# A hybrid encoder of two layers: the builder orders the whole program by a model of five queues, and B's second values are projected ahead of its second queries

## The chip, the cores and the metric

The kernel runs on one core of one Trainium2 chip. The metric is the device time of one execution in microseconds (us). TensorE (PE) multiplies matrices, VectorE (DVE), ScalarE (ACT) and GpSimd (POOL) do the rest, and SyncE (SP) issues the DMAs. Each engine has a queue of its own, and the engines signal each other by semaphores.

## The reference

x has 512 positions of 1024 features, in float32; there are two layers. Cut to what matters:

```python
h = rmsnorm(x, g_attn[l])
qa, ka, va, qb, kb, vb = split(h @ w_in[l])
# q and k: RMSNorm per head of 64, then rotary
ya = windowed_gqa_sink(qa, ka, va, sink[l])     # A: 8 q heads, 2 kv heads, window +-128, a sink logit
yb = diff_attention(qb, kb, vb, lam)            # B: 4 heads, (softmax(q0 k0) - lam softmax(q1 k1)) v
yb = rmsnorm(yb, subln[l]) * (1.0 - lambda_init)
x = x + concat(ya, yb) @ w_out[l]
h = rmsnorm(x, g_ffn[l])
gate, val = split(h @ w_up[l])                  # 2816 columns each
x = x + (silu(centred_dwconv(gate)) * val) @ w_down[l]
```

## The kernel before

Every product of weights is made of three matmuls (`mm3`, L228 to L231): each operand is split into a high part in a shortened float format and a low part, the rest, and high x high, high x low and low x high are added up. Weights come in units (L178 to L194) of 128 partitions x up to 1024 elements by a DMA on SP into two raw buffers; ACT casts the high part and DVE or POOL subtracts the low part (`emit_unit`, L198). `next_unit` keeps up to three units ahead. For the later input weights and the output weights POOL makes the low part in four quarters (L213), for the others DVE does in one piece (L219).

A layer goes in these stages:

- **Projections** (`project`, L355). The columns of w_in are nine chunks of 256 (`CHUNKS`, L29): akv (A's keys and values), aq0 and aq1, then B by halves: bq0, bk0, bv0, bq1, bk1, bv1. Each takes two units and 4 x 8 x 3 = 96 matmuls of 256 columns, and fills two PSUM banks (512 columns of a float each) in turn. The norm's scale per position, na_r, is applied when a bank is emptied: `scaled` (L373) for queries and keys, `v_out` (L437) for values. `qk_out` (L376) then does the norm per head and the rotary (for B on POOL), transposes on PE and splits.
- **Group A**, eight steps of (ip, qb): `a_scores` (sc_a, L507), `a_soft` (exponentials L534, scales L546 and L549), `a_values` (transposes pt_a L578, copies p_a L554 and L556, products pv_a). Four of eight `tmp` buffers belong to a step, so two steps are under way at most.
- **Group B**, sixteen scores of (half, qb, j): `b_scores` (sc_b, L638) into one pair of banks that there is once, `b_soft` (maximum L648, exponentials L654, the difference L663), `b_weights` (transposes wt_b L682), `b_values` (yb), and `b_norm` after every four (ss_yb L721, rr_yb L273, rt_yb L735). The queries and keys of the second half take the buffers of A's queries, so bq1 comes after A's last score.
- **Output projection**: `out_pass` 0 for A, 1 for B's first half, and `out_last` for the second half by halves of the positions (wo, L817).
- **Channel mixer** (L859 to L903): 22 steps of two up products (gate and value, 24 matmuls of 512 columns each) with a chain of nine operations on DVE, ACT and POOL, and two down passes of 8 products. Over both layers that is 88 up units and 64 down units.

The order of the attention part comes from `pump` (L142). The scores, the values and the projections with the output passes (`filler`, L830) are generators; each yields how long it thinks its matmuls took, or a condition on `clk["now"]`. The ready one of lowest rank goes on (values 1, scores 2, filler 3, all side work 0). Blocks of filler are up to 1.45 us long by this clock. What the side work costs on ACT, DVE and POOL stands in `pause` and `mark` as constants. The rest of the program is put out stage by stage in program order. The framework, called with schedule_with_timeline_sim=True (L957), then schedules what it was given; the trace shows single matmuls of one product between those of another.

At the start the squares of the first norm (L254) are scaled by `gate`, a value 1.0 that is computed from the low part of the fourth weight unit (L303), so that they come after it. In layer 0 akv is multiplied slice by slice as x and its weights arrive (L294 to L300).

Of the kernel before, what the change touches and what calls it, by code (L numbers as in the profile page):

```python
# [28 lines left out]
CHUNKS = ("akv", "aq0", "aq1", "bq0", "bk0", "bv0", "bq1", "bk1", "bv1")  # L29
CW = 256  # L30
AHEAD = 3
# [3 lines left out]
FIRST_MM = 1  # L35
N_COL = NK + NK + 3 * NF + NF + 1
N_ROW = 4 * HD + 8 + 4 * HD


@with_exitstack  # L40
def kernel(
# [17 lines left out]
    PSUM = bass.MemoryType.PSUM  # L59

    const = ctx.enter_context(tc.tile_pool(name="const", bufs=1))
# [3 lines left out]
    def pair(name):  # L65
        return sb.tile([P, 2, S], F32R, tag="pair", bufs=8, name=name)

    def keep(name):
        return sb.tile([P, 2, S], F32R, tag="keep", bufs=10, name=name)

    def hid(name, part):
        return sb.tile([P, S], F32R, tag=f"hid{part}", bufs=NK, name=name)

    def prob(name):
        return sb.tile([P, 2, S], F32R, tag="prob", bufs=4, name=name)

    def tmp(name, n=S):
        return sb.tile([P, S + 16], F32, tag="tmp", bufs=8, name=name)[:, :n]

    def rp(name):  # L80
        return sb.tile([P, 2, CW], F32, tag="rp", bufs=RP, name=name)
# [7 lines left out]
    def mm(name):  # L89
        return ps.tile([P, S], F32, tag="mm", bufs=2, name=name)  # L90

    def at(name):
        return ps.tile([P, S], F32, tag="at", bufs=2, name=name)

    def sc2(name):
        return ps.tile([P, 2, S], F32, tag="sc", bufs=1, name=name)

    def accum(name):
        return ps.tile([P, S], F32, tag="acc", bufs=1, name=name)

    def tq(name):
        return ps.tile([P, S], F32, tag="tq", bufs=1, name=name)

    cyc = {"i": 0}

    def wide(name):
        cyc["i"] += 1
        i = cyc["i"] % 5
        return sc2(name)[:, 0] if i == 4 else (mm, at)[i % 2](name)

    def turn(name):
        cyc["i"] += 1
        return (mm, at)[cyc["i"] % 2](name)

    def run(gen):
        for _ in gen:
            pass

    def chain(*gens):
        for g in gens:  # L120
            yield from g


    never = 1e9
    clk = {"now": 0.0}
    due = {}
    tracks = []

    def pause(dt):
        t = clk["now"] + dt  # L130
        return lambda: t

    def when(*names):
        return lambda: max(due.get(n, never) for n in names)

    def mark(name, dt=0.0):
        due[name] = clk["now"] + dt

    def spawn(rank, gen):
        tracks.append([rank, gen, lambda: 0.0])  # L140

    def pump():  # L142
        while tracks:
            ready = [v for v in tracks if v[2]() <= clk["now"]]
            if not ready:
                clk["now"] = min(v[2]() for v in tracks)
                assert clk["now"] < never
                continue
            tr = min(ready, key=lambda v: v[0])
            step = next(tr[1], None)  # L150
            if step is None:
                tracks.remove(tr)
            elif callable(step):
                tr[2] = step
            else:
                clk["now"] += step
                tr[2] = lambda: 0.0
# [9 lines left out]
    ones, nhalf, warm, gate, zero = (unit[:, i:i + 1] for i in range(5))  # L167
# [8 lines left out]

# [18 lines left out]
    state = {"emitted": 0, "used": 0}  # L195
    ready = []
    
    def emit_unit():  # L198
        i = state["emitted"]
        src, (k, n), kind = units[i]  # L200
        raw = sb.tile([P, k, n], F32, tag="wr", bufs=2, name=f"wr{i}")
        hi = sb.tile([P, k, n], F32R, tag="wh", bufs=3, name=f"wh{i}")
        lo = sb.tile([P, k, n], F32R, tag="wl", bufs=3, name=f"wl{i}")
        nc.sync.dma_start(raw, src)
        eng = nc.gpsimd if kind in ("inb", "out") else nc.vector
        if eng is nc.vector:
            split(eng, hi, lo, raw)
        else:
            nc.scalar.copy(hi, raw)  # L209
            q = k // 4  # L210
# [3 lines left out]
        ready.append((hi, lo))  # L214
        state["emitted"] += 1

    def split(eng, hi, lo, raw):
        nc.scalar.copy(hi, raw)  # L218
        eng.tensor_tensor(out=lo, in0=raw, in1=hi, op=ALU.subtract)  # L219

    def next_unit():
        while state["emitted"] < min(len(units), state["used"] + 1 + AHEAD):
            emit_unit()
        u = ready[state["used"]]
        state["used"] += 1
        return u

    def mm3(acc, a, b, start, stop):  # L228
        nc.tensor.matmul(acc, lhsT=a[0], rhs=b[0], start=start, stop=False)  # L229
        nc.tensor.matmul(acc, lhsT=a[0], rhs=b[1], start=False, stop=False)  # L230
        nc.tensor.matmul(acc, lhsT=a[1], rhs=b[0], start=False, stop=stop)  # L231


    class Norm:
        def __init__(self, l, base, name):
            self.l, self.base, self.name = l, base, name
            self.x = []
# [3 lines left out]
            self.part = sb.tile([P, S], F32, tag="tab", bufs=3, name=f"{name}_sum")  # L241

        def add(self, k, x):
            g = cols[:, self.l, self.base + k:self.base + k + 1]
            self.hi[k] = hid(f"{self.name}_h{k}", 0)
            self.lo[k] = hid(f"{self.name}_l{k}", 1)
            nc.scalar.activation(self.hi[k], x, AF.Copy, scale=g)
            nc.vector.scalar_tensor_tensor(out=self.lo[k], in0=x, scalar=g, in1=self.hi[k],  # L248
                                           op0=ALU.mult, op1=ALU.subtract)
            self.x.append(x)  # L250

        def square(self, k):
            sq = self.part if k == 0 else tmp(f"{self.name}_q{k}")
            nc.scalar.activation(sq, self.x[k], AF.Square, **({"scale": gate} if self.first else {}))  # L254
            if k:
                eng = nc.gpsimd if self.base == 0 and not self.first else nc.vector
                eng.tensor_tensor(out=self.part, in0=self.part, in1=sq, op=ALU.add)

        def rms(self):
            acc = accum(f"{self.name}_ss")  # L260
            for t in range(NT):
                nc.tensor.matmul(acc[:, t:t + 1], lhsT=self.part[:, t * P:(t + 1) * P], rhs=ones,
                                 start=True, stop=True)
            v = small(f"{self.name}_v", NT)
            nc.vector.tensor_scalar(out=v, in0=acc[:, 0:NT], scalar1=1.0 / D, scalar2=EPS,
                                    op0=ALU.mult, op1=ALU.add)
            r = small(f"{self.name}_r", NT)
            rsqrt(r, v)
            return r

    def rsqrt(o, i):
        e = nhalf if len(i.shape) == 2 else nhalf.unsqueeze(2)
        nc.gpsimd.tensor_tensor(out=o, in0=i, in1=e.broadcast_to(list(i.shape)), op=ALU.pow)  # L273

    def split_out(hi, lo, src):
        split(nc.vector, hi, lo, src)

    nc.scalar.activation(warm, ones, AF.Copy, scale=ones)
    nc.sync.dma_start(cols[:, :, :N_COL], col_par)
    first_w = [[sb.tile([P, 4, CW], dt, tag=tag, bufs=b, name=f"{tag}_f{i}")  # L280
                for dt, tag, b in ((F32, "prob", 4), (F32R, "wh", 3), (F32R, "wl", 3))] for i in range(2)]
    for k in range(NK):
        nc.sync.dma_start(x_sb[k], x_v[:, k])
        nc.sync.dma_start(first_w[k // 4][0][:, k % 4], units[k // 4][0][:, k % 4])
    state.update(emitted=2, used=2)
    ready.extend([None, None])
    nc.sync.dma_start(ident, ident_in)
    norm = Norm(0, 0, "na0")
    first_banks = []
    for tp in range(2):  # L290
        b = mm(f"pj0_akv_{tp}")
        nc.tensor.matmul(b, lhsT=zero.broadcast_to([P, P]), rhs=zero.broadcast_to([P, S]), start=True, stop=False)
        first_banks += [b[:, i * CW:(i + 1) * CW] for i in range(2)]
    for k in range(NK):  # L294
        norm.add(k, x_sb[k])
# [10 lines left out]
    for k in range(NK):  # L306
        norm.square(k)

    for l in range(depth):
# [19 lines left out]
        if l:  # L329
            make_tabs((2, 3))  # L330
# [130 lines left out]
        def first_part():  # L461
# [7 lines left out]
            else:  # L469
# [5 lines left out]
                for _ in range(3):  # L475
                    yield next(g)
# [496 lines left out]
```

## Time and profile before

| what | us |
|---|---|
| three runs: median (lowest, highest) | 1269.65 (1268.99, 1269.84) |
| the profiled execution, own time | 1269.12 |
| its span, first to last instruction | 1267.3 |
| attention part of layer 0, to the first up product | 0 to 278.1 |
| channel mixer of layer 0 | to 640.8 |
| attention part of layer 1 | to 900.7 |
| channel mixer of layer 1 and the last store | to 1267.3 |

The profile gives the busy time of each engine in a stretch. PEld is the loading of weights into TensorE, which overlaps with PE. PEclk is the share of full clock that TensorE was granted. A row of a group or of the timeline gives the time of one instruction from start to end; matmuls are pipelined, so that a row of 0.39 us can follow the one before it after 0.23. A row of waits reads: who waited for whom, total us, times, longest.

### The profile page before, as it was taken

How to read it: one execution, taken by the hardware profiler on the slowest of the kernel's cores; microseconds unless marked ns; L12 is line 12 of the kernel's file. 1: busy time of each engine (PE TensorE's matmuls, PEld its weight loads, DVE VectorE, ACT ScalarE, POOL GpSimd, SP SyncE). 2: the span in 40 equal slices, each digit the busy share in tenths (PEclk: the TensorE clock that was granted, in tenths of full speed). 3: DMA queues.
4: the chain of work that ended last, by engine and by line, in shares of the span. 5: the costliest groups of instructions: out<-in, count | busy, mean ns of one | idle time of the engine just before them, and what ended most of it. 6: DMA issues, size and time to landing. Idle time of an engine off the chain costs nothing.

```text
span 1267.3 us, 17144 instructions
## 1 busy us (share of the span) xinstructions
PE 1227.2 (97%) x6644; PEld 1034.7 (82%) x6644; DVE 718.9 (57%) x1256; ACT 559.7 (44%) x979; POOL 315.6 (25%) x418
## 2 busy tenths in 40 slices
PE   9897999889999999999999989998999999999998
PEld 8885897778888888888899879876788888888887
DVE  6786665756655334555467667756565543355532
ACT  5576754544433223333346756544443322233321
POOL 1583384201111000112234826631021100011100
PEclk9898999989999999999999989999899999999999
DMA  6221012103332333332332211221133323333232
GB/s 206 73 66 35 15 62 70 64 18 100 100 100 83 93 107 100 101 94 73 103 97 68 67 34 34 67 67 34 34 118 99 100 80 95 110 98 100 81 109 92
DMA packets 33617, 102.93 MB, mean 81 GB/s; under 512 B 3968, under 2 KB 5248, under 8 KB 33536
## 3 DMA queue, kind: packets, MB, share of 16 engines
q1 hardware_dynamic: 33536, 101.84, 26.0%
q8 instruction: 52, 0.85, 0.3%
q14 instruction: 29, 0.24, 0.1%
HBM read 99.73 MB, written 2.10 MB: 80 GB/s over the span
## 4 chain that ended last, share of the span: by engine, by line
PE 93%; DVE 3%; ACT 2%; issue 0%; POOL 0%; DMA 0%; SPq 0%; ACTq 0%; DVEq 0%
PE up L230 13%; PE up L231 13%; PE up L229 12%; PE dn L229 6%; PE dn L231 6%; PE dn L230 6%; PE sc_b L638 2%; PE wo L229 2%; PE wo L230 2%; PE wo L231 2%; PE sc_a L507 2%; PE wo L817 1%; PE pt_a L578 1%; PE pj_aq L229 1%; PE pj_bq L230 1%; PE pj_bk L230 1%
## 5 line engine op out<-in xcount | busy, mean ns | idle before, releaser
L218 ACT CAST wh<-wr 128x1024 fp32r<-128x1024 f32 (+2 forms) x166 | 157.2, 948 | 379.3 <-PE up L230 181.0
L230 PE MATMUL up<-nf_l,wh 128*128 128x512 f32 x704 | 273.5, 389 | 0.4 <-DVE nf_l L248 0.4
L229 PE MATMUL up<-nf_h,wh 128*128 128x512 f32 x704 | 273.6, 390 | 0.0
L231 PE MATMUL up<-nf_h,wl 128*128 128x512 f32 x704 | 273.3, 390 | 0.0
L219 DVE TENSOR_TENSOR wl<-wr,wh 128x1024 fp32r<-128x1024 f32 (+2 forms) x166 | 182.9, 1103 | 115.1 <-ACT wh L218 114.8
L879 POOL TENSOR_TENSOR cv<-cv,rb 128x512 f32<-128x512 f32 x44 | 58.8, 1337 | 514.9 <-ACT cv L878 514.9
L230 PEld LDWEIGHTS up<-nf_l,wh 128*128 128x128 f32 x704 | 132.2, 188 | 28.7 <-DVE nf_l L248 1.3
L231 PEld LDWEIGHTS up<-nf_h,wl 128*128 128x128 f32 x704 | 132.2, 188 | 27.8 <-DVE wl L219 0.3
L229 PEld LDWEIGHTS up<-nf_h,wh 128*128 128x128 f32 x704 | 132.2, 188 | 27.1
L229 PE MATMUL dn<-act,wh 128*128 128x512 f32 x352 | 138.4, 394 | 0.0
L231 PE MATMUL dn<-act,wl 128*128 128x512 f32 x352 | 137.7, 392 | 0.0
L230 PE MATMUL dn<-act,wh 128*128 128x512 f32 x352 | 136.3, 388 | 0.0
L213 POOL TENSOR_TENSOR wl<-wr,wh 128x256 fp32r<-128x256 f32 x144 | 106.1, 770 | 74.7 <-ACT wh L209 74.7
L872 DVE TENSOR_TENSOR gp<-up,rb 128x512 f32<-128x512 f32 x44 | 30.2, 691 | 98.1 <-PE up L231 98.1
L231 PEld LDWEIGHTS dn<-act,wl 128*128 128x128 f32 x352 | 66.1, 188 | 15.5
L230 PEld LDWEIGHTS dn<-act,wh 128*128 128x128 f32 x352 | 66.1, 188 | 14.8
L229 PEld LDWEIGHTS dn<-act,wh 128*128 128x128 f32 x352 | 66.2, 188 | 13.2
L880 DVE TENSOR_TENSOR cv<-cv,up 128x512 f32<-128x512 f32 x44 | 30.2, 686 | 78.7 <-POOL cv L879 69.4
L893 DVE TENSOR_TENSOR x<-x,dn 128x512 f32<-128x512 f32 x32 | 22.1, 690 | 76.4 <-PE dn L231 76.4
L654 ACT ACTIVATE e_b<-sc_b,mx_b,rqb 128x512 f32<-128x512 f32 x64 | 49.4, 777 | 30.9 <-DVE mx_b L649 30.7
L878 ACT ACTIVATE cv<-cv 128x512 f32<-128x512 f32 x44 | 27.6, 631 | 73.6 <-DVE cv L877 73.5
L209 ACT CAST wh<-wr 128x1024 fp32r<-128x1024 f32 x36 | 37.7, 1050 | 21.7 <-PE wo L230 5.2
(226 smaller groups left out, 2516.7 us busy)
## 6 DMA issues: line engine op xcount, KB each, us to landing
wr<-w_up SPq DMA_DIRECT2D x88, 512.0 KB, 3.6
wr<-w_in SPq DMA_DIRECT2D x34, 512.0 KB, 3.6
wr<-w_down SPq DMA_DIRECT2D x32, 384.0 KB, 3.0
wr<-w_down SPq DMA_DIRECT2D x32, 320.0 KB, 2.9
wr<-w_out SPq DMA_DIRECT2D x16, 512.0 KB, 3.5
x<-xT SPq DMA_DIRECT2D x8, 256.0 KB, 4.3
outT<-x SPq DMA_DIRECT2D x8, 256.0 KB, 2.0
prob_f<-w_in SPq DMA_DIRECT2D x8, 128.0 KB, 4.3
```

The lines of the kernel that those rows point to most:

```text
L209: nc.scalar.copy(hi, raw)
L213: eng.tensor_tensor(out=lo[:, o], in0=raw[:, o], in1=hi[:, o], op=ALU.subtract)
L218: nc.scalar.copy(hi, raw)
L219: eng.tensor_tensor(out=lo, in0=raw, in1=hi, op=ALU.subtract)
L229: nc.tensor.matmul(acc, lhsT=a[0], rhs=b[0], start=start, stop=False)
L230: nc.tensor.matmul(acc, lhsT=a[0], rhs=b[1], start=False, stop=False)
L231: nc.tensor.matmul(acc, lhsT=a[1], rhs=b[0], start=False, stop=stop)
L654: nc.scalar.activation(e[c], scp[:, c], AF.Exp, bias=mx[:, c:c + 1], scale=rq[:, c:c + 1], accum_out=lsum[:, c:c + 1])
L872: nc.vector.tensor_tensor(out=g[:, 1:S + 1], in0=acc[0], in1=rb, op=ALU.mult)
L878: nc.scalar.activation(cv, cv, AF.Silu)
L879: nc.gpsimd.tensor_tensor(out=cv, in0=cv, in1=rb, op=ALU.mult)
L880: nc.vector.tensor_tensor(out=cv, in0=cv, in1=acc[1], op=ALU.mult)
```

## The change

The builder no longer puts instructions out as it makes them. Each engine call makes an `Op` that knows what it reads and writes, how long it keeps its engine (`pitch`) and how much later its result is there (`lag`). All work is tracks: generators that yield an Op, or a condition that must hold. `Machine.run` looks at every track's next Op, computes when it could start (its engine free, its operands written, its target read, a shared port of DVE and POOL free), and on each engine takes the lowest rank among those within HOLD of the earliest; the earliest of these over all engines is put out. `tc.manual_schedule()` keeps that order.

```diff
+ctx.enter_context(tc.manual_schedule())
...
+        if self.eng == "PE":
+            if self.name == "transpose" or free_size(writes[0]) <= P:
+                return 0.111, 0.165
...
+            half = reads[0].partition_size() == HD
+            return (n / 2400 + 0.0135) / (2 if half else 1), 0.165
...
+        if self.eng == "ACT":
+            return (n / 1200 + (0.04 if from_ps else 0.09) + 0.09 * scalars
+                    + (0.092 if "accum_out" in self.kw else 0.0), 0.1)
...
+            self.port = sb_in > 1
+            return n / 960 + 0.067 + 0.06 * scalars, 0.085
...
+    def run(self):
+        while self.tracks:
+            best = {}
+            for t in list(self.tracks):
+                while callable(t[3]) and t in self.tracks and t[3]():
+                    self.step(t)
+                if t not in self.tracks or callable(t[3]):
+                    continue
+                s, op = min(((self.when(v), v) for v in (t[3] if isinstance(t[3], tuple) else (t[3],))),
+                            key=lambda v: v[0] + v[1].pitch)
+                best.setdefault(op.eng, []).append((s, t[0](), t[1], t, op))
...
+            for eng, c in best.items():
+                s0 = min(v[0] for v in c)
+                hold = 0.02 if eng == "PE" else HOLD
+                w = min((v for v in c if v[0] <= s0 + hold), key=lambda v: (v[1], v[2]))
+                if pick is None or w[0] < pick[0]:
+                    pick = w
+            s, _, _, t, op = pick
+            self.put(op, s)
+            self.step(t)
```

Ranks: side work of the projections' banks 3, additions to x 4, A's steps 10 to 17, B's scores 30 to 45, the mixer's chains 50 and up, filler 1000; weight units 1, 12 or 400 by how many are ready. Filler yields after each matmul. Loading, cast and low part of the units are three tracks (`w_load`, `w_high`, `w_low`); the low part of input and output units is made in two halves, each on DVE or POOL, whichever would end first:

```diff
-            for j in range(4):
-                o = slice(j * q, j * q + q)
-                eng.tensor_tensor(out=lo[:, o], in0=raw[:, o], in1=hi[:, o], op=ALU.subtract)
...
+            if kind in ("inb", "out", "in"):
+                for j in range(LO_CUT):
+                    o = slice(j * k // LO_CUT, (j + 1) * k // LO_CUT)
+                    yield tuple(e.tensor_tensor(out=lo[:, o], in0=raw[:, o], in1=hi[:, o], op=ALU.subtract)
+                                for e in (dve, pool))
```

The second half's values come ahead of its queries and keys, in the order of the projections and of the weight units:

```diff
-CHUNKS = ("akv", "aq0", "aq1", "bq0", "bk0", "bv0", "bq1", "bk1", "bv1")
+CHUNKS = ("akv", "aq0", "aq1", "bq0", "bk0", "bv0", "bv1", "bq1", "bk1")
...
             yield from proj_b(0)
+            yield from proj_v(0)
+            yield from proj_v(1)
             yield from proj_b(1)
```

The squares of the first norm lose `gate`: they are a track of rank 20 that waits for each slice of x. In layer 0 rope and mask are loaded after the fourth unit, the row parameters after them. The PSUM banks of the output and mixer products go to whichever tag is free first. The operations of the computation, their shapes and the sizes of all buffers stay, except for the halves above.

More of the change, by code (lines that the diff above doesn't have):

```diff
@@ L1 @@
+import heapq
 import math
@@ new lines, in free_size, with places @@
+def free_size(v):
+    n = 1
+    for d in v.shape[1:]:
+        n *= d
+    return n
+def places(v):
+    step, parts = v.ap[0]
+    size = 4
+    if v.space == bass.MemoryType.DRAM:
+        return None
+    first = v.offset % step if step else v.offset
+    p0 = v.base_partition()
+    dims = [(abs(a), n) for a, n in v.ap[1:] if n > 1 and a]
+    lows = [first + sum(a * (n - 1) for a, n in v.ap[1:] if a < 0)]
+    dims.sort()
+    run = 1
+    while dims and dims[0][0] <= run:
+        a, n = dims.pop(0)
+        run = a * (n - 1) + run
+    for a, n in dims:
+        lows = [b + a * i for b in lows for i in range(n)]
+    if v.space == bass.MemoryType.PSUM:
+        return 0, P, tuple(sorted({(b * size // 2048 * 512, b * size // 2048 * 512 + 512) for b in lows}))
+    return p0, p0 + parts, tuple((b, b + run) for b in sorted(lows))
@@ L59 @@
     PSUM = bass.MemoryType.PSUM
+    m = Machine(nc)
+    pe, dve, act, pool, sync = (Queue(e) for e in ("PE", "DVE", "ACT", "POOL", "SP"))
     const = ctx.enter_context(tc.tile_pool(name="const", bufs=1))
@@ L87, in smp, with roomy, any_bank @@
         return sb.tile([P, n], F32, tag="smp", bufs=SMP, name=name)
[L89 to L157, printed above, removed]
+    def roomy(tags):
+        return lambda: any(m.live[t] < m.cap[t] for t in tags)
+    def any_bank(name, tags):
+        tag = min((t for t in tags if m.live[t] < m.cap[t]), key=lambda t: m.slots[t][0])
+        t = new(tag, name)
+        return tag, t, (t[:, 0] if tag == "sc" else t)
     x_sb = [const.tile([P, S], F32, name=f"x{k}") for k in range(NK)]
@@ L166 @@
     unit = const.tile([P, 16], F32, name="unit")
-    ones, nhalf, warm, gate, zero = (unit[:, i:i + 1] for i in range(5))
+    ones, nhalf, warm, zero = (unit[:, i:i + 1] for i in range(4))
     nc.gpsimd.memset(ones, 1.0)
@@ L217, in split, with w_rank, w_load @@
-    def split(eng, hi, lo, raw):
-        nc.scalar.copy(hi, raw)
-        eng.tensor_tensor(out=lo, in0=raw, in1=hi, op=ALU.subtract)
+    raws, his, ready = [], [], []
+    state = {"used": 0}
+    def w_rank():
+        return RK["w"][min(len(ready) - state["used"], 2)]
+    def w_load(first):
+        for i in range(first, len(units)):
+            src, (k, n), kind = units[i]
+            yield m.room("wr")
+            raw = new("wr", f"wr{i}", [P, k, n])
+            yield sync.dma_start(raw, src)
+            raws.append(raw)
@@ L252, in square @@
[L252 to L257, printed above, removed]
+            yield m.room("hid0")
+            self.hi[k] = new("hid0", f"{self.name}_h{k}")
+            yield act.activation(self.hi[k], x_sb[k], AF.Copy, scale=g)
@@ new lines, in add, with squares @@
+            yield m.room("hid1")
+            self.lo[k] = new("hid1", f"{self.name}_l{k}")
+            yield dve.scalar_tensor_tensor(out=self.lo[k], in0=x_sb[k], scalar=g, in1=self.hi[k],
+                                           op0=ALU.mult, op1=ALU.subtract)
+            m.flags.add(f"{self.name}{k}")
+        def squares(self):
+            eng = pool if self.base == 0 and not self.first else dve
+            for k in range(NK):
+                yield m.has(f"{self.name}{k}")
+                if k == 0:
+                    yield m.room("tab")
+                    self.part = new("tab", f"{self.name}_sum", [P, S])
+                    yield act.activation(self.part, x_sb[k], AF.Square)
+                    continue
+                yield m.room("tmp")
+                sq = new("tmp", f"{self.name}_q{k}")
+                yield act.activation(sq[:, :S], x_sb[k], AF.Square)
+                yield eng.tensor_tensor(out=self.part, in0=self.part, in1=sq[:, :S], op=ALU.add)
+                m.drop("tmp", sq)
+            m.flags.add(f"{self.name}_sq")
@@ L264, in rms @@
+            m.drop("tab", self.part)
             v = small(f"{self.name}_v", NT)
[L265 to L284, printed above, removed]
@@ L301 @@
-    emit_unit()
-    emit_unit()
-    nc.vector.tensor_scalar(out=gate, in0=ready[-1][1][:, 0, :1], scalar1=1.0, scalar2=1.0, op0=ALU.max, op1=ALU.min)
-    nc.sync.dma_start(rope_sb, rope)
-    nc.sync.dma_start(mask_sb, mask)
-    for k in range(NK):
-        norm.square(k)
-    for l in range(depth):
+            yield dve.tensor_scalar(out=v, in0=acc[:, 0:NT], scalar1=1.0 / D, scalar2=EPS, op0=ALU.mult, op1=ALU.add)
+            m.drop("acc", acc)
+            self.r = small(f"{self.name}_r", NT)
@@ new lines, with first_norm, first_weights @@
+    first_banks = []
+    def first_norm(norm):
+        for k in range(NK):
+            yield m.has(f"x{k}")
+            yield from norm.add(k)
+    def first_weights():
+        for k in range(NK):
+            yield m.has(f"x{k}")
+            raw, hi, lo = (v[:, k % 4] for v in first_w[k // 4])
+            yield act.copy(hi, raw)
+            yield dve.tensor_tensor(out=lo, in0=raw, in1=hi, op=ALU.subtract)
+            m.flags.add(f"fw{k}")
+            if k % 4 == 3:
+                m.drop("prob", first_w[k // 4][0])
@@ new lines, in first_product @@
+    def first_product(norm):
+        for tp in range(2):
+            b = new("mm", f"pj0_akv_{tp}")
+            yield pe.matmul(b, lhsT=zero.broadcast_to([P, P]), rhs=zero.broadcast_to([P, S]), start=True, stop=False)
+            first_banks.append(b)
+        for k in range(NK):
+            yield m.has(f"fw{k}", f"{norm.name}{k}")
+            hi, lo = (v[:, k % 4] for v in first_w[k // 4][1:])
+            for t in range(NT):
+                yield from mm3(first_banks[t // 2][:, t % 2 * CW:t % 2 * CW + CW],
+                               (norm.hi[k][:, t * P:(t + 1) * P], norm.lo[k][:, t * P:(t + 1) * P]),
+                               (hi, lo), False, k == NK - 1 and t % 2 == 1)
+            if k % 4 == 3:
+                done_with(first_w[k // 4][1:])
+        m.flags.add("first")
@@ new lines, in project, with qk_track, go @@
+                on_bank(tag, bank, tp)
+        def qk_track(nm, tag, bank, tp, tab, dst, rq, rank, is_kv=False):
+            def go():
+                yield m.has(f"{h_in.name}_r")
+                yield m.room("rp", 2)
+                raw = new("rp", f"raw_{nm}{l}_{tp}")
+                sq_t = new("rp", f"sq_{nm}{l}_{tp}")
+                for i in range(2):
+                    yield act.activation(raw[:, i], bank[:, i * CW:(i + 1) * CW], AF.Copy,
+                                         scale=h_in.r[:, 2 * tp + i:2 * tp + i + 1])
+                m.drop(tag, bank)
+                m.spawn(rank, qk_out(nm, raw, sq_t, tp, tab, dst, rq, is_kv))
+            m.spawn(3, go())
@@ L452 @@
[L452 to L460 removed]
+        qa = [(new("pair", f"qah{l}_{i}"), new("pair", f"qal{l}_{i}")) for i in range(2)]
@@ L623, in b_scores @@
             qp, i = qb // 2, 2 * j + qb % 2
-            yield when(f"bq{half}{qp}", f"bk{half}0", f"bk{half}1")
-            yield lambda: 0.0 if used["tmp"] <= 4 else never
-            used["tmp"] += 2
+            yield m.has(f"{lf}bq{half}{qp}", f"{lf}bk{half}0", f"{lf}bk{half}1")
+            yield m.room("tmp", 2, 6)
+            e = [new("tmp", f"e_b{l}_{h}_{qb}_{c}") for c in range(2)]
             if i == 0:
@@ L703, in b_norm @@
+            for v in tiles:
+                m.drop("prob", v)
+            if qp and j:
+                for v in [vb[half, i] for i in range(2)]:
+                    m.drop("keep", v)
         def b_norm(half, qp):
@@ L785, in proj_b @@
-            yield from project(f"bv{half}", lambda bank, tp: bv_done(half, bank, tp), mm)
-            mark(f"vb{half}", 2.0)
-        norm = Norm(l, c0, f"nf{l}")
-        def add_x(d, acc, o):
-            yield pause(0.3)
-            nc.vector.tensor_tensor(out=x_sb[d][:, o], in0=x_sb[d][:, o], in1=acc, op=ALU.add)
-        def out_pass(p, alloc):
+            yield m.room("pair", 4)
+            qk[half] = tuple((new("pair", f"b{n}h{l}_{half}"), new("pair", f"b{n}l{l}_{half}")) for n in "qk")
@@ L796, in out_pass, with add_x @@
+        def add_x(d, tag, bank, o, then=None):
+            w = o.stop - o.start
+            yield dve.tensor_tensor(out=x_sb[d][:, o], in0=x_sb[d][:, o], in1=bank[:, :w], op=ALU.add)
+            m.drop(tag, bank)
+            if then is not None:
+                yield from nf.add(d)
+        def out_pass(p, tags):
             k0, nk = ((0, 4), (4, 2))[p]
-            yield when(*([f"y{ip}{qb}" for ip, qb in a_seq] if p == 0 else ["yb00", "yb01"]))
+            yield m.has(*([f"{lf}y{ip}{qb}" for ip, qb in a_seq] if p == 0 else [f"{lf}yb00", f"{lf}yb01"]))
@@ new lines, in out_last, with rb_track @@
+                m.spawn(4, add())
+            if half:
+                for v in b_st[1, "y"]:
+                    m.drop("keep", v)
+        def rb_track():
+            yield m.has(f"{nf.name}_r")
+            yield m.room("acc")
+            rps = new("acc", f"rps{l}")
+            for t in range(NT):
+                yield pe.matmul(rps[:, t * P:(t + 1) * P], lhsT=nf.r[:, t:t + 1].broadcast_to([P, P]), rhs=ident,
+                                start=True, stop=True)
+            yield m.room("tmp")
+            rb = new("tmp", f"rb{l}")
+            yield act.copy(rb[:, :S], rps)
+            m.drop("acc", rps)
+            b_st["rb"] = rb
+            m.flags.add(f"{lf}rb")
@@ L906, in _lay_out @@
+        m.spawn(5, setup())
+        m.spawn(lambda: score_rank["r"], all_scores())
+        m.spawn(lambda: value_rank["r"], all_values())
+        m.spawn(1000, filler())
+    layer(0, norm)
+    m.run()
+    tc.model = m
 def _lay_out(inp):
```

1067 lines of the change are left out of this document (633 added, 434 removed).

## The prediction

> **What bounds the kernel now.** I read the page first, for the busiest engine.
>
> ```profile
> span 1267.3 us, 17144 instructions
> PE 1227.2 (97%) x6644; PEld 1034.7 (82%) x6644; DVE 718.9 (57%) x1256; ACT 559.7 (44%) x979; POOL 315.6 (25%) x418
> PEclk9898999989999999999999989999899999999999
> ```
>
> TensorE (PE) is busy for 1227.2 of 1267.3 us, the other engines for about half or less. An order of work can therefore only win back what PE loses: 40.1 us of idle time, and the time in which it worked at a lowered clock, the digits below 9. Next I cut the span into stages, to see where those losses lie.
>
> ```profile
> core 0: us, PE busy (x) PEld busy (x) DVE busy (x) ACT busy (x) POOL busy (x), PEclk, DMA share, GB/s
> 31.00:51.00 20.00, 16.64 (x121) 16.44 (x121) 14.83 (x35) 11.08 (x23) 11.28 (x12) 0.83 0.21 74
> 51.00:100.00 49.00, 49.00 (x381) 44.06 (x380) 40.45 (x100) 31.95 (x77) 40.23 (x42) 1.00 0.22 66
> 100.00:136.00 36.00, 27.77 (x153) 20.96 (x152) 25.63 (x80) 26.05 (x67) 5.71 (x8) 0.81 0.10 30
> 136.00:240.00 104.00, 103.87 (x676) 87.34 (x675) 65.24 (x128) 55.54 (x116) 57.82 (x66) 1.00 0.18 57
> 240.00:278.00 38.00, 29.51 (x202) 25.95 (x201) 21.61 (x49) 14.52 (x29) 2.01 (x2) 0.91 0.06 21
> 278.00:640.80 362.80, 362.62 (x1604) 299.22 (x1603) 182.15 (x226) 132.95 (x173) 44.53 (x79) 1.00 0.31 96
> 738.00:762.00 24.00, 18.79 (x117) 15.79 (x116) 14.65 (x45) 16.25 (x41) 5.58 (x8) 0.86 0.15 45
> 860.00:901.00 41.00, 33.08 (x209) 28.65 (x208) 22.81 (x51) 15.37 (x31) 2.02 (x2) 0.83 0.08 26
> ```
>
> The channel mixer of layer 0 (278 to 640.8) has no hole: 362.62 of 362.80 us at full clock. All that matters lies in five stretches of the attention part. For each I take idle time plus busy time x (1 - PEclk): 31 to 51: 3.4 + 2.8 = 6.2 us; 100 to 136: 8.2 + 5.3 = 13.5; 240 to 278: 8.5 + 2.7 = 11.2; in layer 1, 738 to 762: 5.2 + 2.6 = 7.8; 860 to 901: 7.9 + 5.6 = 13.5. Together 52.2 us. The rest of the idle time is mostly the first load and the last store, which no order changes. What PE waits for in these stretches, from the lists of waits of the first three:
>
> ```profile
> PE pj_aq L229 <- ACT raw_kv L373: 3.4, 1, 3.4
> PE pv_a L229 <- ACT p_a L554: 4.7, 2, 3.4
> PE sc_a L507 <- DVE mx_a L511: 3.3, 3, 1.6
> PE rt_yb L735 <- POOL rr_yb L273: 3.2, 2, 1.8
> PE wo L817 <- ACT yh_b L554: 2.1, 2, 1.5
> ```
>
> So there are three kinds of hole: before the first projection can leave its banks (31 to 51), in group A's softmax when no projection is left to fill in (100 to 136, 738 to 762), and in the last normalisation of group B (240 to 278, 860 to 901).
>
> **Part by part. 1: the first norm's squares lose their gate.**
>
> ```profile
> L254 ACT ACTIVATE na_q<-x,unit x7: 707/709/713, 21.6 to 25.3; 128x512 f32<-128x512 f32 x7
> 33.02 1.02 POOL L273 TENSOR_TENSOR na_r<-na_v,unit 128x4 f32<-128x4 f32 x1
> 34.07 0.84 ACT L373 ACTIVATE raw_kv<-pj_akv,na_r 128x256 f32<-128x256 f32 x2 [0.18 <-POOL na_r L273]
> ```
>
> Before, they wait for a weight unit and begin at 21.6. After, each may start when its slice of x is there, behind the casts in rank. Eight squares of 0.71 us fit under the loads that came before 21.6. Then come sum, reciprocal root (1.02) and scale: I put raw_kv at 25 where it was 34.07, an estimate, 9 us earlier (bounds 6 and 10). PE's wait of 3.4 us ended with raw_kv's first scale at about 34.9, so its four banks last to 31.5, later than 25: the 6.2 us of this stretch go whole.
>
> **2: B's second values go ahead of its second queries.** Before, filler runs out in A:
>
> ```profile
> 105.30 0.28 PE L231 MATMUL pj_bv<-wh,na_l 128*128 128x256 f32 x1
> 128.06 0.85 ACT L437 ACTIVATE vb<-pj_bv,na_r 128x256 fp32r<-128x256 f32 x2
> 133.95 0.36 PE L229 MATMUL pj_bq<-wh,na_h 128*128 128x256 f32 x1
> 660.00:670.00 10.00, 10.00 (x87) 10.00 (x86) 8.04 (x15) 5.16 (x9) 3.24 (x3) 1.00 0.28 66
> ```
>
> The first values' projection ends at 105.3, its banks are emptied only at 128, and bq1 starts at 133.95, when A's scores are done. Moving bv1 in puts 4 x 8 x 3 = 96 matmuls there; at 10.00/87 = 0.115 us each that is 11 us of PE work, in holes of 8.2 us (layer 0) and 5.2 us (layer 1), and it keeps the clock up. Both holes are covered: 13.5 and 7.8 us. The same 11 us are missing later, in B's part: that is the step on which all hangs.
>
> **3: B's pace.** B's sixteen scores share one pair of banks, so score follows score: product, maximum, two exponentials.
>
> ```profile
> 136.52 0.89 PE sc_b L638 x5
> 229.42 0.91 PE sc_b L638 x6
> 253.75 0.90 PE sc_b L638 x6
> 762.13 0.89 PE sc_b L638 x6
> 842.82 0.90 PE sc_b L638 x5
> 875.06 0.91 PE sc_b L638 x6
> 278.09 0.39 PE L229 MATMUL up<-nf_h,wh 128*128 128x512 f32 x1
> 900.68 0.40 PE L229 MATMUL up<-nf_h,wh 128*128 128x512 f32 x1
> L648 DVE TENSOR_REDUCE mx_b<-sc_b x32: 1208/1218/1226, 139.1 to 876.0; 128x2 f32<-128x1024 f32 x32
> L654 ACT ACTIVATE e_b<-sc_b,mx_b,rqb x64: 758/779/794, 141.3 to 878.6; 128x512 f32<-128x512 f32 x64
> ```
>
> From first to last score, 15 steps: (253.75 - 136.52)/15 = 7.8 us in layer 0, (875.06 - 762.13)/15 = 7.5 in layer 1. The links themselves take 0.9 + 1.2 + 2 x 0.8 = 3.7, so at least half of each step is waiting in queues. Where filler is thin the old order already goes faster: four steps from 229.42 to 253.75 are 6.1 each, five from 842.82 to 875.06 are 6.4. The new order picks every instruction by the time at which it could start and lets filler in last; bounds are 3.7 and 7.8, and I take 6.4, the slower of the two paces that the trace shows with PE less crowded.
>
> The end of layer 0's attention part (first up product, 278.09) is the later of two: PE's own work, 278.1 - 6.2 - 13.5 - 11.2 = 247.2; and B's chain: first score 9 us earlier at 127.5, 15 x 6.4 = 96, and from the last score to up 278.1 - 253.75 = 24.3, sum 247.8. Layer 1: PE 900.7 - 7.8 - 13.5 = 879.4; chain 762.1 + 96 + 25.6 = 883.7 (A's own pace, which sets the first score, taken as unchanged). As both limits stand within 5 us of each other, waits will not all be covered; I leave 4 us in each layer, an estimate from the 11.2 and 13.5 there now (bounds 0 and those). So 251.8, a gain of 26.3, and 887.7, a gain of 13.0.
>
> That remainder of 4 us holds clock too: in 240 to 278 no single wait is longer than 1.8 us, yet PEclk is 0.91. [...]
>
> **4: weight casts, queues, DMAs.** The low halves of the input and output weights, quarters on POOL before, become halves that go to POOL or DVE, whichever ends first; DVE is busy 65 of 104 us in 136 to 240, so there is room: no cost, and at worst some 1 us for each of 36 units, half of them hidden, +18. On SP the rope, mask and row loads now follow four weight units and bv1's units go ahead of bq1's; with a DMA share of 0.16 to 0.31 I count nothing, and up to +2 if the tables come late. The channel mixer has no hole to lose: 0 (cost bounds under the third rival).
>
> **Sum.** 26.3 + 13.0 = 39.3 us off. The profiled execution took 1269.12 us (span 1267.3 and 1.8 around it; the median of the runs is 1269.65): 1269.1 - 39.3 = 1230.
>
> **Rivals.** (a) *Given back.* B's pace stays at 7.8 and 7.5 because DVE and ACT, not PE's order, set it; the 11 us taken from B's filler reopen as holes. Layer 0: 127.5 + 117.2 + 24.3 = 269.0, a gain of 9; layer 1: nothing. 1260. For it: ACT and DVE together stand at 121 of 104 us in 136 to 240, in one chain; against it: the 6.1 us steps. (b) *All holes close* and A goes faster too: the PE limits of 247.2 and 879.4 give 52.2 us, 1217, and below that some 10 us more if matmuls that now stand alone (0.39 us by their rows against 0.227 back to back in the mixer, 362.8/1604) follow closer: 1207. (c) *Slower: a cast in the wrong place in the channel mixer.* One order is fixed for ACT, by modelled times; if in each of the 44 gate steps the next unit's cast stands behind an activation that waits for DVE, PE waits for it.
>
> ```profile
> L218 ACT CAST wh<-wr 128x1024 fp32r<-128x1024 f32 x102 | 107.0, 1051 | 211.2 <-PE up L230 156.8 <-PE dn L230 25.1 <-DMA wr<-w_up 8.3
> ```
>
> At one cast of 1.05 us for each of 44 steps that is 46 us: 1276. It decides from 39.3/44 = 0.9 us a step. Against it: this cast waits for PE, not PE for it, and 133 of 363 us of ACT are in use. The Trainium skill ("TensorE: Matmul & The Clock Gate", the part on the array's architecture) states that ScalarE and VectorE are strictly first in, first out, which is what this rival needs; no row here speaks against it. (d) *The order on the chip is not the emitted one* and nothing moves: 1269.
>
> **How the numbers follow.** Forecast, 1212 to 1246: 0.60. (b), below 1212: 0.12. (a), 1246 to 1264: 0.16. (d): 0.03. (c), above 1272: 0.09. The range of 1207 to 1262 leaves out half of (b), a tenth of (a), and (c) and (d): 0.2 in all. The limit of 0.2% (2.5 us) is about what a measurement of this kernel can tell from no change; faster 0.87, same 0.04, slower 0.09.
>
> **What would show it.** Step 1: na_r before 26 us and no PE wait on raw_kv. Step 2: PE busy without a hole from 31 to B's first score, pj_bv in one block of two ahead of the second pj_bq. Step 3: steps of sc_b at 6 to 6.8 us; up of layer 0 at 250 +- 6, attention of layer 1 246 us long against 260. Wrong if the steps stay above 7.4 us (rival a), or if PE shows idle time between 300 and 600 (rival c).

## The result and the profile after

The change takes 1307.3 us (median of four runs) against 1269.74 beside it: a ratio of 1.0291, 95% interval 1.0272 to 1.0311. It is slower by 2.9%, where 1230 was forecast. One execution took 5312 us for a cause that is open (a matmul of an up product lasted 1.33 us where 0.39 is usual, at a PEclk shown as 1.00), so the ratio goes by the four others, 1304.92 to 1308.61, and the profile after is that of one more execution (1302.26 us). Its page, first lines:

```profile
span 1300.2 us, 17154 instructions
PE 1241.8 (96%) x6644; PEld 1039.6 (80%) x6644; DVE 753.3 (58%) x1334; ACT 563.0 (43%) x979; POOL 222.4 (17%) x281
PEclk9999999879999999999999999988799999999999
```

The span is 32.9 us longer. DVE has 34 us more work and POOL 93 less (low halves moved over). The stretches, cut at the same events as before (columns: us, busy time of PE, PEld, DVE, ACT, POOL, then PEclk, DMA share, GB/s):

```profile
31.00:47.00 16.00, 16.00 (x135) 15.88 (x134) 9.93 (x22) 6.65 (x14) 4.77 (x5) 1.00 0.27 84
100.00:144.00 44.00, 39.45 (x262) 31.92 (x260) 30.78 (x98) 31.53 (x80) 2.50 (x2) 0.96 0.16 49
144.00:250.00 106.00, 97.52 (x586) 78.91 (x585) 77.53 (x143) 52.44 (x107) 30.26 (x24) 0.95 0.16 51
250.00:291.90 41.90, 31.09 (x189) 26.76 (x189) 21.09 (x45) 15.31 (x29) 2.02 (x2) 0.79 0.00 0
291.90:655.20 363.30, 361.85 (x1602) 298.97 (x1601) 180.18 (x226) 131.75 (x169) 40.51 (x73) 1.00 0.32 96
780.00:893.00 113.00, 102.79 (x605) 82.15 (x604) 80.66 (x148) 55.65 (x115) 29.87 (x24) 0.92 0.17 52
893.00:933.20 40.20, 29.39 (x176) 25.72 (x176) 20.60 (x44) 14.18 (x27) 2.02 (x2) 0.79 0.00 1
```

The channel mixer is as it was (363.3 us against 362.8). All of the loss is in the attention parts: 291.9 us against 278.1 in layer 0, and 933.2 - 655.2 = 278.0 against 259.9 in layer 1, so 13.8 + 18.1 = 31.9. Idle time plus busy time x (1 - PEclk), the measure of the prediction, says where: the hole behind A shrinks from 13.5 to 4.6 + 1.6 = 6.2 us, but the middle of B, which lost 0.1 us, now loses 8.5 + 4.9 = 13.4, and its end 10.8 + 6.5 = 17.3 where it was 11.2. The start, 0 to 31 us, loses 5.2 + 1.5 = 6.7 us where it lost 1.9 (PE busy 25.82 us at 0.94, before 29.11 at 1.00). Two small groups show the start, and B's first and last score in each layer (count: shortest/median/longest ns, first and last start):

```profile
L229 POOL TENSOR_TENSOR na_r<-na_v,unit x1: 1327/1327/1327, 19.9 to 19.9; 128x4 f32<-128x4 f32 x1
L229 ACT ACTIVATE raw_ka<-pj_akv,na_r x4: 466/474/482, 21.3 to 22.4; 128x256 f32<-128x256 f32 x4
L229 PE MATMUL sc_b<-bkh,bqh x2: 496/500/503, 144.1 to 145.2; 64*128 64x512 f32 x2
L229 PE MATMUL sc_b<-bkh,bqh x2: 497/497/497, 264.5 to 264.5; 64*128 64x512 f32 x2
L229 PE MATMUL sc_b<-bkh,bqh x2: 499/500/500, 780.1 to 780.1; 64*128 64x512 f32 x2
L229 PE MATMUL sc_b<-bkh,bqh x2: 497/498/498, 905.4 to 905.4; 64*128 64x512 f32 x2
```

A score of B follows the one before after (264.5 - 144.1)/15 = 8.0 us, in layer 1 after 8.35; before it was 7.8 and 7.5. One step, from the timeline of DVE and ACT (start, duration; in brackets the idle time before it and what ended it):

```profile
228.78 0.69 DVE L229 TENSOR_TENSOR x<-x,wo 128x512 f32<-128x512 f32 x1 [1.06 <-PE wo L229]
229.38 1.22 DVE L229 TENSOR_REDUCE mx_b<-sc_b 128x2 f32<-128x1024 f32 x1
230.60 0.69 DVE L229 TENSOR_TENSOR x<-x,wo 128x512 f32<-128x512 f32 x1
231.21 0.68 DVE L229 TENSOR_TENSOR wl_b<-wt_b,wh_b 128x512 fp32r<-128x512 f32 x1
232.10 0.69 DVE L229 TENSOR_TENSOR x<-x,wo 128x512 f32<-128x512 f32 x1 [0.21 <-PE wo L229]
233.00 1.29 DVE L229 TENSOR_TENSOR wl<-wr,wh 128x512 fp32r<-128x512 f32 x2 [0.21 <-ACT wh L229]
234.21 0.15 DVE L229 SCALAR_TENSOR_TENSOR mx_b<-mx_b,rqb 128x2 f32<-128x2 f32 x1
234.46 0.78 ACT L229 ACTIVATE e_b<-sc_b,mx_b,rqb 128x512 f32<-128x512 f32 x1 [1.49 <-DVE mx_b L229]
236.28 0.50 PE L229 MATMUL sc_b<-bkh,bqh 64*128 64x512 f32 x2
```

The maximum ends at 230.60. The scale that needs nothing else, 0.15 us long, starts 3.6 us later: two additions to x, a low half of the step before and two low halves of a weight unit were put ahead of it. Idle time is only 0.42 of the 3.6; the queue works, on the wrong things. ACT and then PE's next product wait for it. The same links for all 32 steps of both layers, as means from the starts and ends of these instructions in the trace (the last column without the pause between the layers):

| us per step | product's end to maximum | maximum's end to scale | second exponential's end to next product |
|---|---|---|---|
| before | 0.45 | 0.38 | 2.16 |
| after | 0.94 | 1.81 | 0.74 |
| after, steps first on DVE (below) | 0.27 | 0.64 | 1.94 |
| that, old order of projections (below) | 0.29 | 0.57 | 1.02 |

PE does let the next score in sooner, as forecast: 1.42 us less per step. DVE takes back 0.49 + 1.43 = 1.92. (The last column holds pauses between B's halves: two of 5.1 us in the second row, of 20.0 and 28.4 in the third, one of 11.3 in the fourth.)

### The profile page after: what moved, and what is told of

The parts are those of the page before. It is cut to its first block, busy times and chain, and to the rows that moved or that the text cites. A ratio compares the mean times of both kernels' runs of the same rounds, so it can differ in the third digit from the quotient of the medians.

```text
span 5309.9 us, 17154 instructions
## 1 busy us (share of the span) xinstructions
PE 5274.8 (99%) x6644; PEld 3627.4 (68%) x6644; DVE 743.4 (14%) x1334; ACT 571.1 (11%) x979; POOL 215.8 (4%) x281
## 4 chain that ended last, share of the span: by engine, by line
PE 99%; DVE 0%; ACT 0%; issue 0%; POOL 0%; ACTq 0%; DVEq 0%; POOLq 0%
PE up L229 41%; PE dn L229 19%; PE wo L229 8%; PE pj_bv L229 4%; PE pj_bk L229 4%; PE pj_bq L229 4%; PE pj_aq L229 4%; PE pv_a L229 2%; PE sc_b L229 2%; PE pj_akv L229 2%; PE yb L229 2%; PE pt_a L229 2%; PE sc_a L229 2%; PE wt_b L229 1%; PE rt_yb L229 1%; PE ss_yb L229 1%
## 5 line engine op out<-in xcount | busy, mean ns | idle before, releaser
L229 PE MATMUL up<-nf_l,wh 128*128 128x512 f32 x704 | 940.7, 1336 | 0.0
L229 PE MATMUL up<-nf_h,wl 128*128 128x512 f32 x704 | 940.7, 1336 | 0.0
L229 PE MATMUL up<-nf_h,wh 128*128 128x512 f32 x704 | 937.1, 1331 | 0.0
L229 PE MATMUL dn<-act,wh 128*128 128x512 f32 x704 | 779.9, 1258 | 0.0
L229 PEld LDWEIGHTS up<-nf_h,wl 128*128 128x128 f32 x704 | 440.9, 626 | 278.2 <-issue 265.7
L229 PEld LDWEIGHTS up<-nf_l,wh 128*128 128x128 f32 x704 | 437.3, 621 | 281.9 <-issue 281.2
L229 PEld LDWEIGHTS up<-nf_h,wh 128*128 128x128 f32 x704 | 436.3, 620 | 277.1 <-issue 275.8
L229 PEld LDWEIGHTS dn<-act,wh 128*128 128x128 f32 x704 | 393.3, 559 | 280.9 <-issue 280.9
L229 PE MATMUL dn<-act,wl 128*128 128x512 f32 x352 | 443.8, 1261 | 0.0
L229 DVE TENSOR_TENSOR wl<-wr,wh 128x512 fp32r<-128x512 f32 (+3 forms) x245 | 224.4, 931 | 667.6 <-ACT wh L229 571.4
L229 PEld LDWEIGHTS dn<-act,wl 128*128 128x128 f32 x352 | 198.5, 564 | 138.7 <-issue 135.5
```

The lines of the kernel that those rows point to most:

```text
L229: getattr(self.raw[op.eng], op.name)(*op.args, **op.kw)
```

## The experiments

**Two parts, each alone.** The second execution of the change, which gave the profile above (nothing edited; 1302.26 us):

> [...] About 1306 us. Rival c (casts in the wrong place in the channel mixer) expects the mixers at some 381 us each where they were 362.8 and 366.6, the attention parts at or below 278 and 260. Rival a (work given back) expects the mixers unchanged and holes after the last B score; to be slower by 36 it would have to lose 18 more in each attention part than the old order did, so 296 and 278. A third theory, that the modelled order is itself slow in group A or B (a chain that steps more slowly than 11.6 us in A or 7.8 in B), expects the attention parts at 296 and 278 with the holes spread over the steps.

The profile after answers it. The mixers take 363.3 and 367.0 us, so rival c falls. The attention parts come to 291.9 and 278.0, and the losses stand in the middle of B as well as after its last score, as the third theory has it.

Then the new builder with the projections in their old order (the order of the weight units goes with it), and the old builder with the new order:

```diff
-            yield from proj_v(1)
             yield from proj_b(1)
+            yield from proj_v(1)
```

> The changed builder with the old order of the projections: bv1 behind bq1 and bk1 again. If the order of the values is what costs (rival a), this comes back to 1270 or below. If the modelled order of the five queues costs by itself, it stays at 1300 to 1320, and up to 20 us slower than the changed kernel where A's holes open again.

> The old builder with bv1 ahead of bq1 and bk1, nothing else. My prediction's steps 2 and rival a: both holes in A covered (21 us), up to 11 us a layer given back in B: 1249 to 1269. If A's holes are not lack of filler but of banks (the first values' banks are emptied only at 128), this is within 3 us of before.

Measured: 1297.56 (ratio to before 1.0224, 1.0207 to 1.0241) and 1280.88 (1.0085, 1.0070 to 1.0100). So both parts cost: the order of the values about 0.0085 x 1270 = 11 us in the old builder and (1.0291 - 1.0224) x 1270 = 8.5 in the new one, the builder by itself 28. In the old builder the new order doesn't fill A's hole; the stretches and groups of that run:

```profile
100.00:136.00 36.00, 27.77 (x154) 20.68 (x152) 25.15 (x79) 26.05 (x67) 5.70 (x8) 0.81 0.09 32
L437 ACT ACTIVATE vb<-pj_bv,na_r x8: 474/482/511, 126.9 to 157.0; 128x256 fp32r<-128x256 f32 x8
```

PE's 27.77 us at 0.81 are exactly those of before: the first values' banks are emptied only from 126.9 on, and the first matmul of the second values comes at 132.8.

**What in the builder costs?** Theory 1: side work (low halves, copies out of banks, additions to x) has a lower rank number than the steps and goes ahead of them. Theory 2: DVE has too much work since it makes low halves. Theory 3: any order fixed by a model is too rigid. Four runs tell them apart. The emitted order given up, so that the framework schedules again:

```diff
-    ctx.enter_context(tc.manual_schedule())
```

> The changed kernel with the builder's order handed to the framework's scheduler again (the manual schedule is switched off), nothing else. Theory 3 (a fixed emitted order is what costs: the chip runs behind the model, and an instruction that waits holds up ready ones behind it): most of the 27 us that the builder costs beyond the order of the projections come back, 1280 to 1288. Theory 1 (side work of low rank number is put ahead of the chains) and theory 2 (low halves moved from POOL to DVE) both say that the scheduler starts from the same list and the same engines: 1298 to 1310.

A's and B's steps ranked ahead of all side work:

```diff
-        a_rank = {s: 10 + i for i, s in enumerate(a_seq)}
-        b_rank = {s: 30 + i for i, s in enumerate(b_seq)}
+        a_rank = {s: 0.01 * i for i, s in enumerate(a_seq)}
+        b_rank = {s: 0.1 + 0.01 * i for i, s in enumerate(b_seq)}
```

> The changed kernel with the ranks of A's and B's steps below all side work (0 to 0.25 instead of 10 to 45), so that a maximum, an exponential or a copy of a chain goes ahead of a weight's low half, a bank's copy and an addition to x whenever both could start within 0.3 us. Theory 1: B's step falls from 8.0 to about 7.3 us and A's from 12.9 to 11.8, so some 10 us per layer less: 1283 to 1290. Theories 2 and 3: the rank decides only among instructions that the model holds ready at the same time, the waits come from elsewhere: 1300 to 1310.

Low halves on POOL again, and a more cautious model:

```diff
-LO_CUT = 2
+LO_CUT = 4
...
-                                for e in (dve, pool))
+                                for e in ((pool,) if kind != "in" else (dve, pool)))
```

> The changed kernel with the low halves of the later input and the output weights in four quarters on POOL alone, as before, in place of two halves on DVE or POOL; layer 1's first projection also waits in the builder for each slice of the norm, which it did not state. Theory 2: DVE gets back the 34 us that it took over (753 against 719), about two thirds of them within B's chains: 1283 to 1292. Theories 1 and 3: DVE was busy 70% of the time there, its sum isn't the limit: 1298 to 1310.

```diff
+SLACK = {"PE": 7, "ACT": 4, "DVE": 4}
...
         self.pitch, self.lag = self.cost(writes, reads)
+        self.lag *= SLACK.get(eng, 1)
```

> The changed kernel with a more cautious model: the time until a result counts as there is seven times as long after TensorE (1.16 us instead of 0.165) and four times after ACT (0.4) and DVE (0.34), so that an instruction that depends on another engine is put further back in its queue; the same wait in layer 1's first projection as in the run with the low halves on POOL. Theory 3: fewer instructions stand at the head of a queue and wait, B's step falls to 7.4 to 7.7 us: 1283 to 1295. Theories 1 and 2: caution only delays the chains further: 1305 to 1325.

Measured: framework 1283.55 (ratio 1.0097, 1.0081 to 1.0112), steps first 1263.08 (0.9936, 0.9921 to 0.9950), POOL 1308.13 (1.0286, 1.0266 to 1.0305), cautious 1273.98 (1.0023, 1.0013 to 1.0032). Theory 2 falls: DVE is back at 722.6 us busy and nothing is won. Theory 1 was too modest: two lines of ranks win 44 us, more than the builder's whole cost of 28. Theory 3 is borne out in part: another order of the same list, or a more cautious one, brings back 24 and 33 us; why they help wasn't taken apart further and stays open.

**Which queue?** The same ranks on one engine at a time:

```diff
+                r = t[0]()
+                if op.eng in FIRST and r % 1:
+                    r = 0.01 * r - 0.09
```

(with a_rank and b_rank raised by 0.001 to mark the steps; FIRST names the engines)

> The changed kernel with A's and B's steps ranked ahead of all side work on VectorE's queue alone; ranks on the other engines as in the change (and the stated wait in layer 1's first projection). With the steps ahead on all engines it was 1263. Theory 1a (VectorE's queue holds the harm: a maximum or a scale stands behind additions to x and low halves that themselves wait): 1262 to 1275, B's step under 6.5 us. Theory 1b (ScalarE's queue holds it: an exponential stands behind casts and bank copies): 1295 to 1307. If both share it: 1278 to 1292.

> The same on ScalarE's queue alone. Theory 1a: 1295 to 1307. Theory 1b: 1262 to 1275. If both share it: 1278 to 1292.

> The same on VectorE's and ScalarE's queues, while TensorE keeps the ranks of the change (transposes of queries and keys ahead of scores). Theories 1a and 1b: as with all engines, 1258 to 1268, or better, since the second half's queries and keys come earlier and B does not stand for 37 us between its halves. Theory 1c (TensorE's own rank is what counted): above 1285.

Measured: DVE 1267.23 (0.9977, 0.9967 to 0.9986), ACT 1305.15 (1.0290, 1.0264 to 1.0316), both 1264.10 (0.9954, 0.9941 to 0.9968). DVE's queue carries 40 of the 44 us; ACT's ranks are worth nothing by themselves and some 3 us on top of DVE's. The builder's wait in layer 1's first projection is in these three runs, in those with POOL and with the cautious model, in the three below that move one kind of side work, and in the run of 1248.62; it isn't what wins, since the run with ACT has it too and stands at 1.0290 where the change stands at 1.0291. The step in the run with DVE, from the timeline:

```profile
228.62 0.75 DVE L230 SCALAR_TENSOR_TENSOR e_b<-e_b,al_b,e_b 128x512 f32<-128x512 f32 x1
229.40 1.23 DVE L230 TENSOR_REDUCE mx_b<-sc_b 128x2 f32<-128x1024 f32 x1
230.66 0.16 DVE L230 SCALAR_TENSOR_TENSOR mx_b<-mx_b,rqb 128x2 f32<-128x2 f32 x1
230.97 0.69 DVE L230 TENSOR_TENSOR x<-x,wo 128x512 f32<-128x512 f32 x1
231.90 0.69 DVE L230 TENSOR_TENSOR wl_b<-wt_b,wh_b 128x512 fp32r<-128x512 f32 x1 [0.25 <-ACT wh_b L230]
```

The scale follows the maximum at once, and the additions to x come behind it.

**The order of the projections again, with quick steps.** The runs of 1263 and of 1267 with bv1 projected last:

> The steps ahead on all engines, as in the run of 1263, but the second half's values projected last, as before the change. Theory V1 (that order costs 9 us whatever the ranks, as it did in the old builder and in the changed one, since it delays the second half's queries and keys): 1250 to 1256. Theory V2 (it costs only as long as the chains are slow; with quick chains A's holes are there to be filled and B has work enough): 1264 to 1272.

> The steps ahead of side work on VectorE's queue alone, and the second half's values projected last, as before the change. If VectorE's queue is the one that counts whatever the order of the projections: 1248 to 1256 (1267 with the values ahead, less the 9 to 15 us that this order cost in three pairs). If the other queues matter once VectorE's is cured: above 1258.

Measured: 1247.77 (0.9827, 0.9808 to 0.9845) and 1248.62 (0.9825, 0.9810 to 0.9839). Both beat the kernel before by 1.7%. Theory V2 falls: the order costs more than ever, (0.9936 - 0.9827) x 1270 = 14 us and (0.9977 - 0.9825) x 1270 = 19. The last score of B's first half and the first of its second, in layer 0, from the timelines of the run of 1263, then that of 1248:

```profile
175.93 0.50 PE L229 MATMUL sc_b<-bkh,bqh 64*128 64x512 f32 x2
212.88 0.49 PE L229 MATMUL sc_b<-bkh,bqh 64*128 64x512 f32 x2
```

```profile
175.45 0.50 PE L229 MATMUL sc_b<-bkh,bqh 64*128 64x512 f32 x2 [0.45 <-ACT e_b L229]
203.21 0.50 PE L229 MATMUL sc_b<-bkh,bqh 64*128 64x512 f32 x2
```

The first half ends alike. With the values ahead, the second half starts 9.7 us later: its queries and keys stand behind the 11 us of bv1. Within the first half the steps of the run of 1248 are 6.1 us ((175.45 - 132.96)/7; its first score is at 132.96); in the change they are 7.9. Quick steps make B's halves short and the pause between them long: 36.9 us in the run of 1263, 12.6 in the change, from start to start.

**Which side work?** One kind at a time put behind the steps, in the change as it is:

```diff
-RK = {"w": (1, 12, 400), "qkb": (7, 38)}
+RK = {"w": (1, 60, 400), "qkb": (7, 38)}
```

> The changed kernel with one rank changed: loads, casts and low halves of a weight unit rank 60 instead of 12 while one unit is ready (1 as before when none is), so behind A's and B's steps. Theory W (the low halves, 1.1 us each, are the side work that stands ahead of the steps on VectorE): 1265 to 1278. Theory X (it is the additions to x) or Q (the queries and keys): 1298 to 1308. If the kinds share it: 1285 to 1297.

```diff
-                m.spawn(4, add_x(d, tag, acc, slice(0, S)))
+                m.spawn(48, add_x(d, tag, acc, slice(0, S)))
...
-                m.spawn(4, add())
+                m.spawn(48, add())
```

> The changed kernel with the additions of the output products to x, and the second norm's casts that follow them, at rank 48 instead of 4. Theory X: 1265 to 1278, and the gain lies in the second half of B, since there are no such additions earlier. Theories W and Q: 1298 to 1308. If the kinds share it: 1285 to 1297. Slower than 1308 if the banks of the output products then come free too late for TensorE.

```diff
-RK = {"w": (1, 12, 400), "qkb": (7, 38)}
+RK = {"w": (1, 12, 400), "qkb": (28, 46)}
...
-            m.spawn(3, go())
+            m.spawn(3 if nm[1] == "a" else rank, go())
```

> The changed kernel with all work on B's queries and keys behind the steps that run beside it: first half rank 28 (after A, before B) instead of 3 and 7, second half rank 46 instead of 3 and 38. Theory Q: 1265 to 1278, the gain mostly in A's steps. Theories W and X: 1298 to 1308. If the kinds share it: 1285 to 1297.

Measured: 1287.57 (1.0131, 1.0102 to 1.0160), 1283.24 (1.0104, 1.0080 to 1.0127) and 1293.49 (1.0173, 1.0158 to 1.0188). No kind carries it alone: (1.0291 - 1.0131) x 1270 = 20, 24 and 15 us. These add up to 59, more than the 40 that DVE's ranks win together ((1.0291 - 0.9977) x 1270), so the gains overlap; these edits also move the ranks on the other engines. The profiles show that each kind has its own place. The attention part of a layer falls into the time up to B's first score, B's fifteen steps, and the time from the last score to the first up product (layer 0 / layer 1, the latter counted from its first projection; from the starts of sc_b and up in the traces):

| us | to B's first score | B's fifteen steps | last score to up |
|---|---|---|---|
| before | 136.5 / 121.3 | 117.2 / 112.9 | 24.4 / 25.7 |
| after | 144.1 / 124.8 | 120.4 / 125.4 | 27.4 / 27.7 |
| steps first on DVE | 137.3 / 118.4 | 112.4 / 117.9 | 24.6 / 24.9 |
| weight units behind | 145.3 / 124.9 | 114.2 / 117.2 | 27.5 / 27.7 |
| additions behind | 142.6 / 124.8 | 110.3 / 109.8 | 23.6 / 22.3 |
| queries and keys behind | 135.5 / 113.6 | 126.6 / 129.9 | 26.5 / 27.7 |

Of the three kinds, the work on B's queries and keys delays A most (with it behind, B's first score comes 8.6 and 11.2 us sooner than in the change), and the additions delay B most (10.1 and 15.6 us): these are the places that theories Q and X named. With the additions behind, the attention parts are back at the times of before (276.5 and 257.0 us), but each mixer takes 5 us more than in the change (368.8 and 372.1): in layer 0 PE waits 3.2 us there for the second norm's casts, which come behind the additions. This profile is of the fastest of its four runs (1276.15). With the queries and keys behind, B's own steps get longer.

## Why the prediction was wrong

**The step that failed** is this sentence of step 3: "The new order picks every instruction by the time at which it could start and lets filler in last". Filler, the matmuls of rank 1000, does come last, and PE's part of the step fell by 1.42 us. But the side work of that filler on DVE has ranks of 1 to 12 (the front part lists them; only weight units have 400, while two are ready). These are mostly ahead of A's 10 to 17 and always ahead of B's 30 to 45, and the lower rank wins whenever both could start within 0.3 us. Step 3's list of links, "product, maximum, two exponentials", also leaves out the scale, the very link that then stood 3.6 us in DVE's queue. I took the pace of 6.4 from stretches where PE was less crowded and never asked where the chain stands in DVE's queue. Over the fifteen steps 8.0 and 8.35 came. Within the halves the steps are 7.5 to 8.3 us; with the ranks turned round (the run of 1263) they are 5.4 to 6.1.

In the terms of the sum, B's fifteen steps took 24.4 and 29.4 us more than the 96 of the forecast. B's first score, for which A's pace was taken as unchanged, came 16.6 and 3.6 us later than forecast, and the end from last score to up took 3.1 and 2.2 us more. Less the 4 us that were set aside in each layer these are 71 us, the way from 39.3 won to 31.9 lost. What lengthened the end wasn't taken apart. Two small slips change nothing: 362.8/1604 is 0.226, not 0.227, and a gain of 13.0 leaves layer 1's attention part 247 us long, not 246.

**Step 4** put the low halves at no cost because DVE was busy 65 of 104 us. As a sum that was right (moving them back wins nothing), as an argument it wasn't: in the change DVE is busy 77.5 of 106 us in the middle of B, and with a quarter of its time free its queue still held a link of 0.15 us back for 3.6 us.

**Step 1** held for its own hole: na_r comes at 19.9 against a forecast of before 26, and 31 to 47 is full (16.00 of 16.00 at full clock). But 0 to 31, where it counted no cost, lost 4.8 us more than before; PE's longest wait there, 2.1 us, is for the cast of a weight unit. The first score of A is only 4 us earlier (47.2 against 51.2, from the trace). A's scores then took 90.6 us from first to last where they took 81.6 before, and 70.2 with the steps first on DVE: A was slowed like B. So B's first score came at 144.1, where 127.5 was forecast and 136.5 was the old time.

**Step 2** failed in its sign. The hole behind A did close by half, but the bill that the text named ("the same 11 us are missing later") was 8.5 to 19 us in four pairs of runs. Two things are shown: with the old builder bv1 starts only at 132.8, after the banks are emptied, so that the hole stays and bq1 starts at 153.2 where it was 133.9; and with quick steps the second half's queries come late.

**The rivals.** (c) had an in-order queue with work in the wrong place, but in the channel mixer and on ACT; the mixer lost nothing, and ACT's ranks alone changed nothing. What it described happened on DVE in the attention part. The Trainium skill ("TensorE: Matmul & The Clock Gate", the part on the array's architecture), cited for it, says that ScalarE and VectorE are strictly first in, first out. The traces agree: the scale stands 3.6 us behind what was emitted ahead of it, and 0.03 us where it was emitted next. (a) was right that holes would move from A into B, and too mild: it kept B's pace at the old value. (b) needed all holes closed, and B's middle opened a new one of 13.4 us. (d) is refuted, since an edit of ranks moves the time by 44 us. The sum's idea that PE's losses could be won back was sound: with the ranks turned round and the projections in their old order the builder reaches 1248, a gain of 22 us where 39 was forecast, and without step 2.

## What to carry to other kernels

When a builder fixes the order of in-order queues, follow the limiting chain through every queue that it passes and list what may stand ahead of each link: here free time on an engine said nothing about the place in its queue. Rank the links of the chain ahead of the side work of filler on VectorE first, and only then judge where filler should go. Work moved into an early hole delays what was next in that order, so ask which chain waits for that.

## What the runs showed of the hardware that was not expected

An operation of DVE with two inputs in SBUF could take longer while POOL was at work. The group of B's differences in the profile after:

```profile
L229 DVE SCALAR_TENSOR_TENSOR e_b<-e_b,al_b,e_b x32: 745/752/1802, 153.1 to 911.8; 128x512 f32<-128x512 f32 x32
```

Of the 32, the 21 with no POOL operation beside them take 0.75 us each. Of the eleven that POOL overlaps, six take 1.07 to 1.80 and five stay at 0.75. The Trainium skill ("Trainium Architecture — The Big Picture", "What this means for kernel authors") calls the port pair of DVE and GpSimd an exclusive lock. The six longer ones agree with that; three of the five others, with POOL beside them for 0.8 us, don't show it.
